# One core's hybrid S5 / RG-LRU / GLA block: more stream before the first head's transposes, a query block before z, the first norm reordered, third products at the turn

## The chip, the cores and the metric

The kernel runs on one core of a Trainium2 chip. The metric is the device time of one execution in microseconds (us), lower is better; a profile is one execution taken by the hardware profiler. Engines: PE is TensorE (matrix products), DVE is VectorE, ACT is ScalarE, POOL is GpSimd, and SP (SyncE) issues nearly all loads.

## What is computed

One block of a sequence model with 1024 latent tokens, 256 context tokens and 1024 channels, in fp32. Cut to its steps:

```python
u  = modulate(rms_norm(h, ln1_g), mod[0], mod[1])        # mod = silu(c) @ ada_w + ada_b, six parts
uc = modulate(rms_norm(hc, ln1_g), mod_c[0], mod_c[1])   # the context, its own modulation
z  = u @ w_in; zc = uc @ w_in                            # 5408 columns: S5, LRU x and gate, q, k, v, g, z, gates
s5  = s5_branch(...)       # two directions, complex diagonal scan, GELU, GLU
lru = rglru_branch(...)    # conv, sigmoid gates, two scans
gla = gla_branch(...)      # four heads, chunks of 64, decays from z
m = g[0] * (s5 @ w_br_s5) + g[1] * (lru @ w_br_lru) + g[2] * (gla @ w_br_gla)
h = h + mod[2] * (m @ w_out)
u = modulate(rms_norm(h, ln2_g), mod[3], mod[4])
h = h + mod[5] * conv_ffn(u, w_up, conv_w, conv_b, w_down)
return rms_norm(h, final_g)
```

Each mixer scans the context first and starts the latent scan from that state.

## The kernel before

Channels lie on partitions, tokens run along the free axis in two halves of 512 (j = 0, 1). Every fp32 product is three products of rounded parts: high by high, low by high, high by low (`uh`, `ul` the normed input, `wh`, `wl` a weight; the low part of a weight is a subtraction on POOL or DVE, line 221, the high part a cast on ACT, line 220). Raw weights come through two buffers (`wr`), high and low parts through three each.

**PE's order is the order of the code** (`manual_schedule` for PE). The large projections are a generator, `proj_stream`, that yields products block by block: latent blocks (`lat`), context blocks (`ctx`), value blocks (`v_steps`), the z blocks that feed the GLA decays (`z_steps`), gates and branch products. The recurrent parts are serial chains through PE, ACT, DVE and POOL; between their steps the code calls `F(name)`, which takes products worth so many us, from the table `FILL`, from the stream. A product of 512 columns counts 0.216 us there. After the last head, `fill(1e9)` takes what is left of the stream; then the merge (line 1568 ff.) multiplies the GLA output, read back from DRAM as `y0` to `y3` and split into parts, by its branch weights.

On DVE, ACT, POOL and SP a scheduler sets the order from PE's order and dependences, except in three stretches that are written out: the start of the program, where the table `START` lists the steps in the order in which every engine gets them, and two stretches around the second norm and the turn to the FFN.

The steps of `START` (methods of `Start`): `x` loads a part of the input, `sq` squares it on ACT, `sa` adds the square to the sum (on DVE, or on POOL if listed in `ONPOOL`), `rs` sums over partitions on PE, `re` and `rp` make the inverse root (DVE, then POOL's power), `rb` broadcasts it with PE, `rc` copies it. `a(r, k)` loads a piece of the modulation weights of part r, `ar(r)` multiplies it with the condition (64 small products), `at` copies the row, `ac` transposes it on PE, `am` makes scale and shift (lines 365 to 367). `un`, `u`, `ul` make the scaled input, its high part (ACT, line 323) and its low part; `m1` and `m2` are the first products of the stream's blocks that run inside the norm (line 434 ff.), `g`, `gh`, `gl` their weights.

The four places: the first head's transposes are line 1347, fed by DVE's line 1323; the z products are line 711, the value blocks' copies out of PSUM line 746, the query blocks' line 580, the LRU's sigmoid `lz` line 1000; at the turn, `q[0]` and `q[1]` are FFN products of the first two channel groups, `p3` their third products (bank `bkc`), `p4` their fourth (bank `bkd`, line 853 ff.).

Of the kernel before, what the change touches and what calls it, by code (L numbers as in the profile page):

```python
# [109 lines left out]
def tile_kernel(tc, I, out, dbg=None):  # L110
# [645 lines left out]
    def proj_stream():  # L756
# [1577 lines left out]
```

## Time and profile before

| | |
|---|---|
| median of 3 runs | 1577.93 us (1577.77 to 1577.96) |
| the profiled execution | 1578.69 us, its span 1576.6 us |
| PE busy | 1513.6 us, 96% of the span |
| DVE, ACT, POOL busy | 1096.1 (70%), 772.3 (49%), 414.6 us (26%) |
| PE's mean granted clock | 0.985 of full speed |

Times of rows count from the start of the span. A row of a timeline gives start, duration, engine, line, operation, the operands by the program's names without buffer numbers (out<-in), and in brackets how long the engine stood idle before it and who released it. Rows with a count join neighbours of one kind. A window's row gives the length, then for each engine its busy time and instructions, then the granted TensorE clock (1.00 is 2.4 GHz, 0.50 is 1.2 GHz), the busy share of the DMA engines and GB/s.

### The profile page before, as it was taken

What the parts mean: (1) busy time and instruction counts of PE and PEld (TensorE: products, weight loads), DVE (VectorE), ACT (ScalarE), POOL (GpSimd) and SP (SyncE); (2) the same over time, 40 slices, a digit from 0 to 9 for tenths busy, and PEclk for the clock granted to TensorE, in tenths of its full rate; (3) what the DMA queues carried; (4) which work ended last, traced back from release to release, by engine and by line L of the source; (5) the groups of instructions that cost most, each with busy time, mean ns of one, the idle gap of its engine ahead of it and who ended that gap; (6) DMA issues with size and microseconds to landing.
All of it is one profiled execution on the core that took longest, in us unless ns stands there. A gap on an engine that the chain in (4) does not pass through costs nothing. (4 is left out here: it accounts for less than half of the span.)

```text
span 1576.6 us, 21571 instructions
## 1 busy us (share of the span) xinstructions
PE 1513.6 (96%) x8144; PEld 1248.9 (79%) x8144; DVE 1096.1 (70%) x1645; ACT 772.3 (49%) x1223; POOL 414.6 (26%) x266
## 2 busy tenths in 40 slices
PE   5999989999996999999999989999999999999997
PEld 4788768877885888888888867778888888878887
DVE  3624379999858434642451899888888888899962
ACT  4523776785534543441332565444444444544661
POOL 2313210011124222222236335333333333000032
PEclk9999999999998999999999999999999999999998
DMA  9764533332224244131574411222222223964303
GB/s 327 256 213 132 187 129 105 117 101 59 59 67 134 77 135 148 70 88 63 172 239 145 141 60 54 94 81 80 81 81 83 93 92 109 371 240 141 101 20 107
DMA packets 93865, 199.04 MB, mean 126 GB/s; under 512 B 13505, under 2 KB 34881, under 8 KB 93633
## 3 DMA queue, kind: packets, MB, share of 16 engines
q1 hardware_dynamic: 82048, 181.75, 34.3%
q10 hardware_dynamic: 11712, 15.91, 2.9%
q8 instruction: 64, 1.05, 0.3%
q14 instruction: 41, 0.33, 0.1%
HBM read 159.11 MB, written 38.52 MB: 125 GB/s over the span
## 5 line engine op out<-in xcount | busy, mean ns | idle before, releaser
L221 POOL TENSOR_TENSOR wl<-wr,wh 128x1024 fp32r<-128x1024 f32 (+1 forms) x78 | 164.2, 2105 | 477.1 <-ACT wh L220 432.8
L220 ACT CAST wh<-wr 128x1024 fp32r<-128x1024 f32 (+2 forms) x87 | 77.1, 891 | 146.2 <-issue 41.3
L221 POOL TENSOR_TENSOR wp<-tmp,wp 128x512 fp32r<-128x512 f32 x44 | 75.2, 1726 | 217.6 <-ACT wp L220 217.6
L534 PE MATMUL ma<-uh,wh 128*128 128x512 f32 x272 | 116.9, 430 | 0.7 <-ACT pt L809 0.7
L534 PE MATMUL mb<-uh,wh 128*128 128x512 f32 x272 | 106.7, 392 | 0.0
L536 PE MATMUL ma<-ul,wh 128*128 128x512 f32 x272 | 106.7, 392 | 0.0
L536 PE MATMUL mb<-ul,wh 128*128 128x512 f32 x272 | 106.7, 392 | 0.0
L538 PE MATMUL mb<-uh,wl 128*128 128x512 f32 x272 | 106.2, 391 | 0.0
L538 PE MATMUL ma<-uh,wl 128*128 128x512 f32 x272 | 105.9, 389 | 0.0
L220 ACT CAST wp<-tmp 128x512 fp32r<-128x512 f32 x78 | 46.5, 619 | 91.4 <-DVE tmp L1648 91.2
L1714 DVE SCALAR_TENSOR_TENSOR ca<-gv,vec,ca 128x1023 f32<-128x1023 f32 (+2 forms) x66 | 62.2, 967 | 23.8 <-ACT ca L1706 23.6
L220 ACT CAST wp<-hd 128x512 fp32r<-128x512 f32 x88 | 52.8, 618 | 49.4 <-PE bkd L2023 26.3
L220 ACT CAST wp<-wr 128x512 fp32r<-128x512 f32 x97 | 58.2, 620 | 32.5 <-DMA wr<-in_wdn_dram 17.1
L1717 DVE SCALAR_TENSOR_TENSOR ca<-gv,vec,ca 128x1023 f32<-128x1023 f32 (+2 forms) x66 | 71.1, 1100 | 0.1
L1378 DVE SCALAR_TENSOR_TENSOR gl<-gl,gl 128x128 f32<-128x128 f32 x72 | 31.2, 433 | 53.1 <-ACT gl L1376 35.6
L534 PEld LDWEIGHTS ma<-uh,wh 128*128 128x128 f32 x272 | 51.3, 189 | 15.4 <-issue 5.2
L221 DVE TENSOR_TENSOR wp<-hd,wp 128x512 fp32r<-128x512 f32 x88 | 60.8, 708 | 1.2 <-ACT wp L220 1.0
L538 PEld LDWEIGHTS ma<-uh,wl 128*128 128x128 f32 x272 | 51.2, 188 | 11.3
L536 PEld LDWEIGHTS ma<-ul,wh 128*128 128x128 f32 x272 | 51.2, 188 | 11.3
L536 PEld LDWEIGHTS mb<-ul,wh 128*128 128x128 f32 x272 | 51.2, 188 | 11.2
L538 PEld LDWEIGHTS mb<-uh,wl 128*128 128x128 f32 x272 | 51.1, 188 | 11.4
L534 PEld LDWEIGHTS mb<-uh,wh 128*128 128x128 f32 x272 | 51.4, 189 | 9.6 <-issue 1.4
(643 smaller groups left out, 4606.3 us busy)
## 6 DMA issues: line engine op xcount, KB each, us to landing
wa<-in_ada_dram SPq DMA_DIRECT2D x96, 256.0 KB
wr<-in_wup_dram SPq DMA_DIRECT2D x46, 512.0 KB
wr<-in_win_dram SPq DMA_DIRECT2D x40, 512.0 KB
wr<-in_wdn_dram SPq DMA_DIRECT2D x22, 512.0 KB
hd<-hid SPq DMA_DIRECT2D x22, 512.0 KB
hid<-ca SPq DMA_DIRECT2D x21, 512.0 KB
wr<-in_wout_dram SPq DMA_DIRECT2D x16, 512.0 KB
tmp<-in_wdn_dram SPq DMA_DIRECT2D x22, 256.0 KB
```

Of the source, the lines that this page charges most:

```text
L220: S.copy(h, src)
L221: lo.tensor_tensor(l, src, f32(h), OP.subtract)
L534: PE.matmul(p[j], h[:, kk], uh[j][:, k], start=f, stop=False)
L536: PE.matmul(p[j], h[:, kk], ul[j][:, k], start=False, stop=False)
L538: PE.matmul(p[j], l[:, kk], uh[j][:, k], start=False, stop=e)
L1378: self.last = V.scalar_tensor_tensor(Sd[:, step], Sd[:, step - 1], self.dec[:, step:step + 1], Sd[:, step], OP.mult, OP.add)
L1714: V.scalar_tensor_tensor(a[:, t0_ + 1:t0_ + 1 + n1], x[:, o:o + n1], fw[0], a[:, t0_ + 1:t0_ + 1 + n1], OP.mult, OP.add)
L1717: V.scalar_tensor_tensor(a[:, t0_ + c - 1:t0_ + n - 1], x[:, o + c:o + n], fw[2], a[:, t0_ + c - 1:t0_ + n - 1], OP.mult, OP.add)
```

## The change

It does four things, and takes no arithmetic away.

- `START` is written in another order, and `ar` is split: pieces 0 to 5 of a part's products stand apart from pieces 6 and 7. The first part's six pieces now come before the broadcast `rb(0)`, the second part's before the second column sums `rs(1)`; the latent halves of input tiles 2 and 3 for j = 0 get their `un`, `u`, `ul` before those for j = 1; the later squares of the second half come after the first `m1`. `ONPOOL` is gone, so `sa` for k = 2, 4, 6 of the second half is on DVE. The square of tile 2 gets a buffer of its own; `sp` and `sf` are not called.
- The second query block (`qsp[1]`, weight 6) moves from before the key blocks of the context to after the first value blocks, right ahead of `z_steps`; its weight moves in the list of loads with it.
- `F("gtr0")`, 13.0 us of stream, ahead of the first head's transposes.
- `q[1].p3()` moves ahead of `q[0].p4()`.

```diff
@@ -72,6 +72,7 @@
         'glu': [22.0],
+        'gtr0': [13.0],
         'gtr': [3.37, 4.7, 3.88, 4.43],
@@ -83,8 +84,7 @@
-ONPOOL = [('sq', 2, 1), ('sq', 4, 1), ('sq', 6, 1)]
...
@@ -308,10 +308,11 @@
-    def ada_rows(r, p):
-        for k, w in enumerate(ada.pop(r)):
+    def ada_rows(r, p, k0=0, k1=KT):
+        for k in range(k0, k1):
+            w = ada[r][k]
@@ -338,8 +339,8 @@
-        def ar(r):
-            ada_rows(r, psm[:, r * 128:(r + 1) * 128])
+        def ar(r, k0, k1):
+            ada_rows(r, psm[:, r * 128:(r + 1) * 128], k0, k1)
@@ -387,12 +388,21 @@
-                t = sqs[k, j] = t0([128, 512], "sq", 3)
+                t = sqs[k, j] = t0([128, 512], "sq" if k != 2 else "sqp", 3 if k != 2 else 1)
...
-            (G if ("sq", k, j) in ONPOOL else V).tensor_tensor(accs1[j], accs1[j], sqs[k, j], OP.add)
+            V.tensor_tensor(accs1[j], accs1[j], sqs[k, j], OP.add)
@@ -762,18 +772,18 @@
-        wsrc.extend([win[i] for i in (35, 36, 37, 0, 5, 6, 3, 4)] + vsrc)
+        wsrc.extend([win[i] for i in (35, 36, 37, 0, 5, 3, 4)] + vsrc + [win[6]])
...
-        for b in range(2):
-            yield from lat(lambda p: out_rows(p, qsp[b]))
+        yield from lat(lambda p: out_rows(p, qsp[0]))
         for b in range(2):
             yield from ctx(lambda p: out_rows([p], ksp[b]))
         yield from v_steps([0, 1])
+        yield from lat(lambda p: out_rows(p, qsp[1]))
         yield from z_steps()
@@ -1495,6 +1505,7 @@
         if h == 0:
+            F("gtr0")
             F("gtr")
             head.transposed()
@@ -1914,10 +1925,10 @@
+    q[1].p3()
     q[0].p4()
     q[0].gate()
     q[0].out()
-    q[1].p3()
     q[1].p4()
```

Lines after the first hunk move by 1 to 11 (the broadcast copy of the first norm and what follows): line 1347 is line 1357 of the changed kernel.

How the instructions move, at three places.

**ACT ahead of the z products.** `lz` is the LRU's sigmoid, `lt` and `lw` its gates and decays, `pt` a copy out of PSUM (a value block's on line 746 before; the query block's on line 590 of the change), the row of line 707 or 717 the copy of the first z product. Before:

```order
L982 ACTIVATE lw313_2045<-la312_2042 128x1280
L972 ACTIVATE lt306_1980<-sm310_2024,hba_1480 128x512
L220 CAST wh386_2345<-wr385_2343 128x1024
L220 CAST wh389_2351<-wr388_2349 128x1024
L972 ACTIVATE lt306_1980<-sm311_2039,hba_1480 128x256
L984 ACT_TABLE_LOAD
L984 ACTIVATE lw313_2045<-lw313_2045 128x1280
L746 COPY pt315_2059<-mb308_1990 128x512
L972 ACT_TABLE_LOAD
L972 ACTIVATE lt314_2052<-sm317_2073,hba_1480 128x512
L747 DMA vsp_681<-pt315_2059 128x2x256
```

Now:

```order
L982 ACTIVATE lt307_2011<-sm308_2018,hba_1480 128x512
L1010 ACTIVATE lz295_1925<-lz295_1925 128x1024
L992 ACTIVATE lw312_2048<-la311_2045 128x1280
L982 ACTIVATE lt307_2011<-sm309_2033,hba_1480 128x512
L590 COPY pt314_2056<-ma299_1938 128x512
L590 COPY pt315_2059<-mb300_1939 128x512
L982 ACTIVATE lt307_2011<-sm310_2042,hba_1480 128x256
L994 ACT_TABLE_LOAD
L994 ACTIVATE lw312_2048<-lw312_2048 128x1280
L591 DMA qsp_680<-pt314_2056 128x512
L591 DMA qsp_680<-pt315_2059 128x512
L982 ACT_TABLE_LOAD
```

The value block's copy stood behind two casts, the table load and the square root; the query block's two copies stand before table load and root, and the two casts (`wh386`, `wh389`) have gone further up.

**PE ahead of the first head's transposes** (line 1347, now 1357; `ma`, `mb` the two halves of a stream block, `sm` the transposes). Before:

```order
L538 MATMUL ma912_4943<-uh0_109,wl870_4766 128x512
L538 MATMUL mb913_4944<-uh1_110,wl870_4766 128x512
L1347 MATMUL sm915_4964<-con_71,gl899_4909 128x128 x4
L1347 MATMUL sm916_4970<-con_71,gl899_4909 128x128 x4
L1347 MATMUL sm917_4976<-con_71,gl899_4909 128x128 x2
L534 MATMUL ma912_4943<-uh0_109,wh869_4765 128x512
```

Now, the last six rows before the first stream block ends and the next begins, and the rows at the transposes:

```order
L546 MATMUL ma912_4943<-ul0_111,wh869_4765 128x512
L546 MATMUL mb913_4944<-ul1_112,wh869_4765 128x512
L548 MATMUL ma912_4943<-uh0_109,wl870_4766 128x512
L548 MATMUL mb913_4944<-uh1_110,wl870_4766 128x512
L544 MATMUL ma919_5005<-uh0_109,wh876_4825 128x512
L544 MATMUL mb920_5006<-uh1_110,wh876_4825 128x512
```

```order
L548 MATMUL ma919_5005<-uh0_109,wl877_4826 128x512
L548 MATMUL mb920_5006<-uh1_110,wl877_4826 128x512
L1357 MATMUL sm922_5038<-con_71,gl899_4909 128x128 x4
L1357 MATMUL sm923_5044<-con_71,gl899_4909 128x128 x4
L1357 MATMUL sm924_5050<-con_71,gl899_4909 128x128 x2
L544 MATMUL ma919_5005<-uh0_109,wh876_4825 128x512
```

Before, 18 stream products stood between the S5 output's products and the transposes, all of one block; now 78 stand there, 48 that end this block and 30 of the next, with the next weight.

**DVE in the first norm** (`mods` scale and shift, `x` the scaled input, `ul` the low part, rows on line 395, now 396, the sums of squares of the second half). Before:

```order
L347 COPY t046_249<-sm12_126 128x128
L395 TENSOR_TENSOR t044_243<-t044_243,t045_247 128x512
L365 TENSOR_TENSOR mods_124<-sm11_125,ab1_104 128x4
L366 TENSOR_TENSOR mods_124<-mods_124,vec_69 128x4
L367 TENSOR_TENSOR mods_124<-sm11_125,vec_69 128x4
L320 SCALAR_TENSOR_TENSOR x1_89<-x1_89,mods_124,t025_139 128x512
L320 SCALAR_TENSOR_TENSOR x2_90<-x2_90,mods_124,t025_139 128x512
L395 TENSOR_TENSOR t044_243<-t044_243,t048_257 128x512
L326 SCALAR_TENSOR_TENSOR ul0_111<-x1_89,mods_124,uh0_109 128x512
L326 SCALAR_TENSOR_TENSOR ul0_111<-x2_90,mods_124,uh0_109 128x512
```

Now:

```order
L396 TENSOR_TENSOR t044_233<-t044_233,t045_237 128x512
L348 COPY t047_253<-sm12_126 128x128
L396 TENSOR_TENSOR t044_233<-t044_233,t046_251 128x512
L366 TENSOR_TENSOR mods_124<-sm11_125,ab1_104 128x4
L367 TENSOR_TENSOR mods_124<-mods_124,vec_69 128x4
L368 TENSOR_TENSOR mods_124<-sm11_125,vec_69 128x4
L321 SCALAR_TENSOR_TENSOR x1_89<-x1_89,mods_124,t025_139 128x512
L321 SCALAR_TENSOR_TENSOR x2_90<-x2_90,mods_124,t025_139 128x512
L327 SCALAR_TENSOR_TENSOR ul0_111<-x1_89,mods_124,uh0_109 128x512
L327 SCALAR_TENSOR_TENSOR ul0_111<-x2_90,mods_124,uh0_109 128x512
L396 TENSOR_TENSOR t044_233<-t044_233,t048_273 128x512
L396 TENSOR_TENSOR t044_233<-t044_233,t049_276 128x512
```

A sum no longer stands between the scaled inputs and their low parts, and all sums of the second half from k = 3 on stand in one row behind them.

## Rows read from the trace of the kernel before

**Rows 1.** PE's waits over the whole run: line, releaser, us in total, times, longest.

```profile
PE sm L1347 <- DVE gl L1323: 12.6, 1, 12.6
PE ma L434 <- ACT uh L323: 4.9, 1, 4.9
PE mb L711 <- ACT pt L746: 4.8, 1, 4.8
```

**Rows 2.** Windows of core 0: busy us per engine, granted PEclk, DMA share, GB/s.

```profile
27.20:32.20 5.00, 4.94 (x12) 3.89 (x13) 2.71 (x4) 2.16 (x6) 1.42 (x2) 0.50 1.05 387
215.70:220.00 4.30, 4.30 (x10) 2.27 (x10) 3.81 (x2) 2.17 (x3) 0.00 (x0) 0.50 0.47 166
509.70:513.50 3.80, 3.76 (x14) 3.47 (x15) 3.35 (x2) 0.97 (x3) 2.68 (x1) 0.50 0.12 13
953.50:957.20 3.70, 3.70 (x10) 2.92 (x11) 3.58 (x5) 3.11 (x5) 3.70 (x4) 0.57 0.00 0
40.00:60.00 20.00, 19.07 (x139) 15.36 (x140) 19.93 (x30) 10.04 (x18) 8.65 (x7) 1.00 0.95 342
280.00:300.00 20.00, 20.00 (x144) 17.33 (x143) 20.00 (x36) 12.72 (x21) 1.98 (x2) 1.00 0.31 105
```

**Rows 3.** PE's timeline at the first head's transposes: start us, us, line, operands, idle before.

```profile
492.83 0.39 PE L534 MATMUL ma<-uh,wh 128*128 128x512 f32 x1
...
496.70 0.39 PE L538 MATMUL mb<-uh,wl 128*128 128x512 f32 x1
509.74 2.39 PE L1347 MATMUL sm<-con,gl 128*128 128x128 f32 x10 [12.65 <-DVE gl L1323]
```

**Rows 4.** POOL's timeline, the next stream weight's split.

```profile
484.31 2.71 POOL L221 TENSOR_TENSOR wl<-wr,wh 128x1024 fp32r<-128x1024 f32 x1 [8.73 <-ACT wh L220]
```

**Rows 5.** PE's timeline at the first product of the merge.

```profile
770.78 0.39 PE L290 MATMUL mm<-y0h,wh 128*128 128x512 f32 x1
```

**Rows 6.** DVE's timeline, the low parts of the merge's third and fourth operands.

```profile
761.44 1.23 DVE L221 TENSOR_TENSOR y2l<-yr,y2h 128x1024 fp32r<-128x1024 f32 x1 [1.88 <-DMA wr<-in_wbr_dram]
764.79 1.23 DVE L221 TENSOR_TENSOR y3l<-yr,y3h 128x1024 fp32r<-128x1024 f32 x1 [2.12 <-ACT y3h L220]
```

**Rows 7.** ACT's timeline before the second z product.

```profile
205.12 1.06 ACT L1000 ACTIVATE lz<-lz 128x1024 f32<-128x1024 f32 x1 [3.48 <-DVE lz L999]
...
215.06 0.57 ACT L746 COPY pt<-mb 128x512 f32<-128x512 f32 x1
```

**Rows 8.** PE's timeline, the second z product.

```profile
215.68 0.69 PE L711 MATMUL mb<-uh,tmp 128*64 128x512 f32 x1 [4.78 <-ACT pt L746]
```

**Rows 9.** DVE's timeline, two weight splits in the LRU.

```profile
211.29 2.36 DVE L221 TENSOR_TENSOR wl<-wr,wh 128x1024 fp32r<-128x1024 f32 x2
```

**Rows 10.** PE's timeline at the start of the program.

```profile
15.85 2.07 PE L279 MATMUL sm<-con,t 128*128 128x128 f32 x8 [1.35 <-POOL t L408]
17.85 3.64 PE L316 MATMUL sm<-wa,c 128*32 128x128 f32 x64
...
27.26 0.80 PE L434 MATMUL ma<-uh,wh 128*128 128x512 f32 x1 [4.86 <-ACT uh L323]
```

**Rows 11.** DVE's timeline at the start of the program.

```profile
22.63 1.25 DVE L366 TENSOR_TENSOR mods<-mods,vec 128x4 f32<-128x4 f32 x1
23.80 0.15 DVE L367 TENSOR_TENSOR mods<-sm,vec 128x4 f32<-128x4 f32 x1
...
25.25 0.68 DVE L395 TENSOR_TENSOR t<-t,t 128x512 f32<-128x512 f32 x1
```

**Rows 12.** ACT's timeline at the start of the program.

```profile
25.96 0.63 ACT L391 ACTIVATE t<-x 128x512 f32<-128x512 f32 x1 [1.44 <-DVE t L395]
```

**Rows 13.** PE's timeline at the turn to the FFN.

```profile
953.48 0.47 PE L853 MATMUL bkd<-T4h,wp 128*128 128x512 f32 x1 [3.15 <-DVE gv L1688]
```

**Rows 14.** ACT's timeline at the turn to the FFN.

```profile
952.53 0.58 ACT L1684 COPY gv<-bkc 128x512 f32<-128x512 f32 x1
```

**Rows 15.** SP's timeline, weight loads of the LRU's end.

```profile
212.54 32.41 SPq L211 DMA_DIRECT2D wr<-in_wv_dram  x4
```

More of the change, by code (lines that the diff above doesn't have):

```diff
@@ new lines @@
+START = [('x', 0, 0), ('sq', 0, 0), ('x', 1, 0), ('sq', 1, 0), ('x', 2, 0), ('sq', 2, 0), ('sa', 1, 0), ('x', 3, 0), ('sq', 3, 0), ('sa', 2, 0), ('x', 4, 0), ('sq', 4, 0), ('sa', 3, 0), ('x', 5, 0), ('sq', 5, 0), ('sa', 4, 0), ('x', 6, 0), ('sq', 6, 0), ('sa', 5, 0), ('x', 7, 0), ('sq', 7, 0), ('sa', 6, 0), ('sa', 7, 0), ('rs', 0), ('a', 0, 0), ('a', 0, 1), ('a', 0, 2), ('a', 0, 3), ('a', 0, 4), ('a', 0, 5), ('ar', 0, 0, 6), ('re', 0), ('rp', 0), ('a', 0, 6), ('a', 0, 7), ('g', 0), ('gh', 0, 0), ('rb', 0), ('gh', 0, 1), ('gl', 0, 0), ('gh', 0, 2), ('x', 0, 1), ('sq', 0, 1), ('gl', 0, 1), ('x', 1, 1), ('sq', 1, 1), ('gl', 0, 2), ('ar', 0, 6, 8), ('rc', 0), ('sa', 1, 1), ('x', 2, 1), ('sq', 2, 1), ('at', 0), ('ac', 0), ('sa', 2, 1), ('am', 0), ('un', 0, 0), ('un', 1, 0), ('u', 0, 0), ('u', 1, 0), ('ul', 0, 0), ('m1', 0, 0), ('ul', 1, 0), ('x', 3, 1), ('sq', 3, 1), ('x', 4, 1), ('sq', 4, 1), ('sa', 3, 1), ('m2', 0, 0), ('x', 5, 1), ('sq', 5, 1), ('m1', 1, 0), ('sa', 4, 1), ('x', 6, 1), ('sq', 6, 1), ('sa', 5, 1), ('x', 7, 1), ('sq', 7, 1), ('a', 1, 0), ('a', 1, 1), ('a', 1, 2), ('a', 1, 3), ('a', 1, 4), ('a', 1, 5), ('ar', 1, 0, 6), ('sa', 6, 1), ('sa', 7, 1), ('m2', 1, 0), ('a', 1, 6), ('a', 1, 7), ('g', 1), ('gh', 1, 0), ('gh', 1, 1), ('gl', 1, 0), ('ar', 1, 6, 8), ('gh', 1, 2), ('rs', 1), ('at', 1), ('gl', 1, 1), ('gl', 1, 2), ('ac', 1), ('re', 1), ('rp', 1), ('am', 1), ('a', 2, 0), ('a', 2, 1), ('a', 2, 2), ('a', 2, 3), ('a', 2, 4), ('a', 2, 5), ('ar', 2, 0, 6), ('un', 2, 0), ('un', 3, 0), ('u', 2, 0), ('rb', 1), ('u', 3, 0), ('ul', 2, 0), ('a', 2, 6), ('a', 2, 7), ('g', 2), ('gh', 2, 0), ('ul', 3, 0), ('gh', 2, 1), ('gl', 2, 0), ('gh', 2, 2), ('ar', 2, 6, 8), ('rc', 1), ('gl', 2, 1), ('m1', 2, 0), ('at', 2), ('un', 0, 1), ('gl', 2, 2), ('un', 1, 1), ('u', 0, 1), ('ac', 2), ('m2', 2, 0), ('un', 2, 1), ('u', 1, 1), ('a', 3, 0), ('a', 3, 1), ('a', 3, 2), ('a', 3, 3), ('a', 3, 4), ('a', 3, 5), ('ar', 3, 0, 6), ('am', 2), ('u', 2, 1), ('ul', 0, 1), ('m1', 0, 1), ('ul', 1, 1), ('ul', 2, 1), ('a', 3, 6), ('a', 3, 7), ('g', 3), ('gh', 3, 0), ('gh', 3, 1), ('ar', 3, 6, 8), ('gl', 3, 0), ('un', 3, 1), ('gh', 3, 2), ('m2', 0, 1), ('gl', 3, 1), ('at', 3), ('u', 3, 1), ('un', 4, 0), ('m1', 1, 1), ('gl', 3, 2), ('ul', 3, 1), ('u', 4, 0), ('ac', 3), ('un', 5, 0), ('m2', 1, 1), ('am', 3), ('u', 5, 0), ('m1', 3, 0), ('ul', 4, 0), ('ul', 5, 0), ('m1', 2, 1), ('un', 4, 1), ('un', 5, 1), ('u', 4, 1), ('m2', 3, 0), ('un', 6, 0), ('u', 5, 1), ('m2', 2, 1), ('ul', 4, 1), ('u', 6, 0), ('m1', 3, 1), ('ul', 5, 1), ('ul', 6, 0), ('m1', 4, 0), ('un', 7, 0), ('m2', 3, 1), ('un', 6, 1), ('u', 7, 0), ('m2', 4, 0), ('un', 7, 1), ('u', 6, 1), ('m1', 5, 0), ('ul', 7, 0), ('u', 7, 1), ('ul', 6, 1), ('m1', 4, 1), ('ul', 7, 1), ('m2', 5, 0), ('m2', 4, 1), ('m1', 5, 1), ('m1', 6, 0), ('m2', 5, 1), ('m2', 6, 0), ('m1', 6, 1), ('m2', 6, 1), ('mz',)]
@@ L394, in sa, with sp, sf @@
         def sa(k, j):
-            (G if ("sq", k, j) in ONPOOL else V).tensor_tensor(accs1[j], accs1[j], sqs[k, j], OP.add)
+            V.tensor_tensor(accs1[j], accs1[j], sqs[k, j], OP.add)
+        @staticmethod
+        def sp(k, j):
+            G.tensor_tensor(sqs[2, j], sqs[2, j], sqs[k, j], OP.add)
+        @staticmethod
+        def sf(j):
+            Start.sa(2, j)
         @staticmethod
```

1 line of the change is left out of this document (removed).

## The prediction

> **What bounds the kernel now.** I read the page's busy shares first: TensorE (PE) is busy 96% of a span of 1576.6 us, so everything that this change can win is in the other 4%, some 63 us, and in stretches where PE's clock is at the lower of its two levels. The view of PE's waits comes next; three of its rows stand where the change does something [rows 1]: 12.6 us before the first head's transposes (on VectorE, DVE), 4.9 us before the first product of the first norm and 4.8 us before the second z product (both on ScalarE, ACT). Third, the granted clock by stretch [rows 2]: 0.50, which is 1.2 of 2.4 GHz, in the 5.0 us after the second of these waits, the 4.3 us after the third and the 3.8 us after the first. A 512-column product moves on by 0.228 us at full clock (492.83 to 496.70, 17 steps [rows 3]), and at half clock takes twice that, so half of each stretch is lost: 2.5, 2.15 and 1.9 us. Last, the timelines of PE and of the engines it waits for at each place.
>
> PE's order is written by hand, so products are not re-sorted at run time: a wait removed in front of PE shortens the whole as long as the engines behind it move along.
>
> **C, 13 us of stream ahead of the first head's transposes.** Before, PE runs out of stream 18 products after 492.83, and waits 12.65 us to 509.74 for DVE's product at L1323 [rows 3]. The change puts 60 more products there, 60 x 0.228 = 13.7 us; they end at 492.83 + 78 x 0.228 = 510.6, 0.9 us after the transposes could begin. Thirty of the 60 use the weight tile that is in use, thirty the next one, which POOL split at 484.31 in 2.71 us [rows 4]. ACT, DVE and POOL keep their order up to the transposes, so DVE's chain stays where it is. The wait of 12.65 us goes and the 1.9 us of half clock behind it: 14.5 us at most. None of it shows at the place: it comes back after the last head, where 60 products less are left to drain.
>
> What is late next is the merge. After the last head 126 stream products stood before the merge, now 66. The merge started at 770.78 [rows 5] and would start 13.7 us earlier, at 757.1 of that clock. Its third and fourth operands y2l and y3l were split by DVE at 761.44 and 764.79, 1.23 us each [rows 6], 4.8 us before the merge began. A step of the merge is six products, 1.37 us, and the low operand is the second product of its step, so they are wanted at 757.1 + 2 x 1.37 + 0.23 = 760.1 and 761.4. With the old times PE would stand until 766.0: 4.6 us in all. SyncE (SP) now has no weight load between the store of the last head and the loads of y, so these go out about 1 us earlier, and y3 needs no weight load to pass; but one weight load, waiting for a split on GpSimd (POOL), now stands ahead of that store. Bounds 0 and 4.6; I take 2.0. **C: 14.5 - 2.0 = 12.5 us.**
>
> **B, one query block between value products and z.** Before, the last block ahead of z is a value block; its copy out of PSUM stands on ACT behind the LRU's casts, a table load and a square root, and starts at 215.06 only [rows 7]. PE needs that buffer for its second z product at 215.68 - 4.78 = 210.9 [rows 8]. After the change the block ahead of z is the query block, and its two copies stand ahead of table load and root. What can still hold them is the LRU's sigmoid `lz`, which ACT ran at 205.12 after waiting 3.48 us for DVE [rows 7]: two weight splits, 2.36 us together [rows 9], now stand on DVE ahead of the scans that feed it. Then `lz` would start at 207.5 and, with 1.06 for itself and about 3 us for the two LRU steps and two copies that follow, the second copy ends near 211.6, against a need at 210.9: 0.7 us of wait. If DVE has the splits done in its own idle time it is 0. I take 0.4. The 2.15 us of half clock go with the wait. **B: 4.8 + 2.15 - 0.4 = 6.5 us**; bounds 0 (copies late after all) and 7.
>
> **A, the first norm.** Before: the broadcast of the root starts at 15.85, the 64 small products of the first modulation part at 17.85, they take 3.64 us and end at 21.49; the first product of the norm comes at 27.26, after 4.86 us of idle [rows 10]. Now 48 of the 64 go ahead of the broadcast, while POOL's power runs: 14.5 (15.85 - 1.35, where the column sums end) + 48/64 x 3.64 = 17.2, broadcast 2.0, the last 16 0.9: 20.1, 1.4 us earlier. From there to the first product it took 27.26 - 21.49 = 5.8 us. In it DVE's L366 took 1.25 us where its neighbours take 0.15 [rows 11], beside a sum on POOL that the change takes from there (1.1 us), and ACT put a Square at 25.96 ahead of the first u, which waited for a sum of DVE that ended at 25.93 [rows 11, 12]; the u steps now stand ahead of those squares (some 1.9 us). So the first product comes about 1.4 + 1.1 + 1.9 = 4.4 us earlier. SP's loads keep their order. Three sums of 0.68 us move from POOL to DVE [rows 11], 2.0 us, and DVE is busy 19.93 of 20 us from 40 to 60 [rows 2], so part of the gain may end there: -1 to 5; nearest is the 4.4 less half of the sums. **A: 3.5 us.** The idle ahead of the product shrinks from 4.86 to about 2.9 us, and I keep half clock behind it, since 3.15 us of idle at the turn [rows 13] were followed by a granted 0.57 [rows 2].
>
> On that clock the Trainium skill ("TensorE: Matmul & The Clock Gate", section "What's actually happening") says that the throttled state is the default and that sustained activity releases it. Both rows agree with that; they don't settle whether 2.9 us with small products around them is idle enough, so the other outcome is a rival below, worth the 2.5 us lost there before.
>
> **D, the third products of the second pair ahead of the fourth of the first.** PE waits 3.15 us to 953.48 [rows 13]. The third products that now come first write the bank that ACT copies out at 952.53 for 0.58 us [rows 14], and use a weight split that ends a little later. So PE waits to 953.1 at the earliest and some 954 at the latest; DVE has work waiting in either order. **D: -0.3 us**, bounds -0.9 and +0.4.
>
> **Give-back.** A and B bring PE to the S5 stage 10 us earlier. DVE is busy 20.00 of 20 us at 280 to 300 [rows 2] and PE has almost no wait there; DVE's chain begins on a load that SP issues behind weight loads, one of which now stands later, so it should start as much earlier. I take 1 us lost, bounds 0 and 10.
>
> **Sum.** 3.5 + 6.5 + 12.5 - 0.3 - 1.0 = 21.2 us. The profiled execution took 1578.69 us, so 1557.5; it lies 0.76 above the median of the runs (1577.93), so I predict 1556.7 us. A measurement of this kernel can tell about 0.2% from no change, 3.2 us.
>
> **Rivals.**
> 1. *The merge stands.* y2 and y3 come as late as before, 4.6 us, and half clock after it costs another 1 (3.7 us at 0.57 after the turn's wait lost 1.6 [rows 2]): 3.6 us worse, 1560.3. For it: both splits were late already [rows 6]. Against: the loads are issued earlier. 0.13.
> 2. *The first norm gives nothing*, because DVE, full from 40 to 60, or the transfers, 0.95 of their share there [rows 2], set its end: 1560.2. 0.11.
> 3. *All of it is hidden, and the first norm keeps the full clock*: A 4.4 + 2.5, B 7, C 14.5, nothing given back: 28.4 us, 1549.5. The clock rule named above is the reason for its 2.5. For it: the gap is shorter than any that half clock follows in rows 2. 0.07.
> 4. *S5 does not move*: DVE starts its chain when it did, and the 10 us of A and B become a wait of PE: 1566. Against: DVE's order there has nothing new. 0.04.
> 5. *Slower.* The two weight splits that now stand ahead of the LRU's scans on DVE wait for late weight loads; scans, sigmoid, copies, z and S5 all queue behind them. One weight load in this place did stand 32.41 us in SP's group of issues [rows 15]. It makes the change slower than before from a lateness of 21.2 + 3.2 = 24.4 us. Against: in SP's order the two loads now stand ahead of that wait. At 30 us: 1587; from 18 to 24 us there would be no difference. 0.04.
> 6. *The extra stream is not there in time*: the products put ahead of the transposes wait for weights or for PSUM, and C is worth nothing: 1569. Against: the split of rows 4 ends long before 503, where the second thirty begin. 0.01.
>
> **How the numbers follow.** The forecast has 0.60. Rivals 1 and 2 lie at 1560, both together near 1564, and rival 3 at 1549.5; the range from 1551.0 to 1564.5 takes in the forecast with the bounds of C and A, and rivals 1 and 2. Left out are 3, 4, 5 and 6, 0.16. Faster by over 0.2%: all but 5, 0.96; of rival 5, 0.01 within 0.2% and 0.03 slower.
>
> **What would show it.** Right: no wait on the transposes of the first head over 2 us and a granted 1.00 around them; no wait of 4.8 us on the second z product; the first product of the norm near 23 us; a new wait of 1 to 3 us on y2l or y3l in the merge; an unchanged wait near 3 us at the turn, now on third products. Wrong: a wait on the transposes as long as A and B together (S5 did not move), over 4 us at the merge, or a first product of the norm after 25 us.

## The result and the profile after

| | before | after |
|---|---|---|
| median of 4 runs each, side by side | 1577.95 us (1577.77 to 1578.85) | 1555.95 us (1553.71 to 1556.22) |
| ratio, 95% interval | | 0.9856 [0.9839, 0.9873] |
| profiled execution | 1578.69 us | 1556.22 us |

22.0 us faster, 1.4%; the forecast was 1556.7, the range 1551.0 to 1564.5. PE has 3.2 us less work in the records and 19 us less idle time. The page after, span and busy times:

```profile
span 1554.4 us, 21567 instructions
PE 1510.4 (97%) x8144; PEld 1244.1 (80%) x8144; DVE 1090.0 (70%) x1648; ACT 774.7 (50%) x1223; POOL 403.1 (26%) x263
```

PE's waits after (in total, times, longest); the rows to compare with are [rows 1]:

```profile
PE bkc L863 <- ACT gv L1695: 2.8, 1, 2.8
PE bkb L864 <- DVE wp L221: 2.4, 1, 2.4
PE ma L444 <- ACT uh L324: 2.4, 1, 2.4
...
PE sm L291 <- DVE s L225: 1.6, 1, 1.6
...
PE mm L290 <- ACT y2h L220: 1.0, 1, 1.0
```

The wait on the transposes (12.6, now L1357) and the one on the second z product (4.8, now L721) are gone, the first norm's (L444) is half as long, and the merge (`mm`) has waits that it hadn't. L291's wait on `s`, the end of S5, was 1.1 before: 0.5 us of what S5 takes back.

PE's order is rigid, so the same instruction can be found in both traces. Its start before less its start after is the lead, and where the lead changes, the time was won or lost:

| PE instruction | before | after | lead |
|---|---|---|---|
| first product of the first norm | 27.26 | 22.82 | 4.44 |
| start of the stream behind the norm | 72.48 | 68.31 | 4.17 |
| second z product | 215.68 | 205.53 | 10.15 |
| first modulation product behind z | 221.84 | 210.08 | 11.76 |
| a middle S5 block | 465.07 | 453.34 | 11.73 |
| stream ahead of the transposes | 492.83 | 481.59 | 11.24 |
| merge, first product | 770.78 | 744.56 | 26.22 |
| merge, second block | 776.27 | 753.16 | 23.11 |
| first FFN products | 920.92 | 897.75 | 23.17 |
| last product | 1568.09 | 1545.29 | 22.80 |

So in this pair of profiles A gave 4.2, B 7.6, S5 took back 0.5, C gave 15.0 to the merge's first product and the merge took back 3.1, and the turn and all behind it changed the time by 0.4. The granted clock after, by stretch (length, PE busy, clock, DMA share, GB/s), against [rows 2]:

```profile
22.80:25.60 2.80, 2.78 (x7) 0.50 1.05 386
200.00:220.00 20.00, 19.56 (x144) 1.00 0.35 128
500.00:520.00 20.00, 19.86 (x128) 1.00 0.41 138
740.00:760.00 20.00, 17.75 (x75) 1.00 0.57 193
930.00:935.00 5.00, 4.79 (x14) 0.66 0.00 0
```

Of the stretches at half clock one is gone at z and one at the transposes, the first norm's is 2.8 us long and no longer 5.0, and the turn's has stayed.

**C at its place.** PE's timeline after, answering to [rows 3]:

```profile
499.30 1.25 PE L1357 MATMUL sm<-con,gl 128*128 128x128 f32 x10
```

DVE's product, the releaser of the wait before, ran here:

```profile
496.54 2.18 DVE L1333 TENSOR_TENSOR gl<-gl,gl 128x1280 f32<-128x1280 f32 x1 [2.75 <-ACT gl L1326]
```

It ends at 498.72, PE arrives at 499.30: 0.6 us late, where 0.9 was worked out.

**The merge.** PE after, where [rows 5] had no wait:

```profile
744.56 0.39 PE L290 MATMUL mm<-y0h,wh 128*128 128x512 f32 x1
...
747.08 0.40 PE L292 MATMUL mm<-y1h,wl 128*128 128x512 f32 x1
748.46 0.51 PE L290 MATMUL mm<-y2h,wh 128*128 128x512 f32 x1 [0.98 <-ACT y2h L220]
749.77 0.50 PE L291 MATMUL mm<-y2l,wh 128*128 128x512 f32 x1 [0.81 <-DVE y2l L221]
...
751.90 0.50 PE L291 MATMUL mm<-y3l,wh 128*128 128x512 f32 x1 [0.47 <-DVE y3l L221]
```

The brackets add up to 2.26 us, but the block takes 3.11 us longer than before. A bracket counts from the modelled end of the product ahead, which is longer (0.39) than the step to the next (0.23): 747.08 to 748.46 is 1.38, so 1.15 is lost where the bracket shows 0.98. SP after, in the same place:

```profile
734.07 1.58 SPq L1560 DMA_DIRECT2D yr<-yosp  x2
...
743.87 1.55 SPq L1560 DMA_DIRECT2D yr<-yosp  x2
```

y0 and y1 are loaded at 734.07; y2 and y3 only at 743.87, since `yr` has two buffers and DVE split the first of them at 742.61 for 1.23 us. The prediction named SP's queue and the weight load in it as what holds these loads; it was the buffers. (In the kernel before it was both: y2's load went out at 755.67, at the end of the first of these splits, y3's at 758.17, behind a weight load.)

**B at its place.** ACT after, against [rows 7]:

```profile
199.93 1.04 ACT L1010 ACTIVATE lz<-lz 128x1024 f32<-128x1024 f32 x1
...
204.47 0.60 ACT L590 COPY pt<-mb 128x512 f32<-128x512 f32 x1
```

The second copy ends at 205.07 and the second z product starts at 205.53 without a wait. `lz` came 5.2 us earlier than before, 1.0 more than A's lead at the stream. The two weight splits that moved ahead of the scans on DVE did take their time, but it came back. DVE after, with the two splits and the product behind the scans:

```profile
191.20 1.22 DVE L221 TENSOR_TENSOR wl<-wr,wh 128x1024 fp32r<-128x1024 f32 x1
...
192.94 1.20 DVE L221 TENSOR_TENSOR wl<-wr,wh 128x1024 fp32r<-128x1024 f32 x1
...
196.90 1.22 DVE L1012 TENSOR_TENSOR lt<-lt,lt 128x1024 f32<-128x1024 f32 x1
```

The same product before, and the weight split that POOL ran beside it:

```profile
199.27 2.87 POOL L221 TENSOR_TENSOR wl<-wr,wh 128x1024 fp32r<-128x1024 f32 x1 [4.09 <-ACT wh L220]
199.98 3.24 DVE L1002 TENSOR_TENSOR lt<-lt,lt 128x1024 f32<-128x1024 f32 x1
```

From DVE's product ahead of the scans (L986, now L996, at 195.34 and 189.79) to their end (199.95 and 196.40) it takes 6.6 us now and took 4.6 before: the splits cost 2.0. The product behind the scans takes 1.22 us and no longer 3.24, because POOL splits nothing beside it: 2.0 won. In noB and onlyC (below), where the query block stands in its old place, it took 3.2 us beside a POOL split again, in all other runs 1.2 without one.

### The profile page after: what moved, and what is told of

Same layout as the page of the kernel before. It is cut to its first block, busy times and chain, and to the rows that moved or that the text cites. A ratio compares the mean times of both kernels' runs of the same rounds, so it can differ in the third digit from the quotient of the medians.

```text
span 1554.4 us, 21567 instructions
## 1 busy us (share of the span) xinstructions
PE 1510.4 (97%) x8144; PEld 1244.1 (80%) x8144; DVE 1090.0 (70%) x1648; ACT 774.7 (50%) x1223; POOL 403.1 (26%) x263
## 5 line engine op out<-in xcount | busy, mean ns | idle before, releaser
L221 POOL TENSOR_TENSOR wl<-wr,wh 128x1024 fp32r<-128x1024 f32 (+1 forms) x78 | 160.9, 2064 | 450.4 <-ACT wh L220 426.6
```

Source lines behind the costliest of these rows:

```text
L221: lo.tensor_tensor(l, src, f32(h), OP.subtract)
```

## The experiments

Eleven runs; the totals in one table, each against runs of the kernel before on the same chip. A median of 4 runs is good to about 0.15%, 2.5 us, so what is smaller is read from the leads at the place and not from totals.

| run | median (range) us | ratio to before [95%] |
|---|---|---|
| noA | 1557.21 (1556.66 to 1560.82) | 0.9874 [0.9857, 0.9891] |
| noB | 1562.70 (1561.15 to 1565.51) | 0.9904 [0.9886, 0.9921] |
| noC | 1568.93 (1568.14 to 1571.09) | 0.9944 [0.9930, 0.9958] |
| noD | 1556.90 (1553.96 to 1556.99) | 0.9863 [0.9846, 0.9879] |
| onlyC | 1563.69 (1562.94 to 1565.34) | 0.9918 [0.9905, 0.9932] |
| g8 | 1570.30 (1569.68 to 1572.47) | 0.9963 [0.9950, 0.9977] |
| g16 | 1568.79 (1565.99 to 1570.44) | 0.9941 [0.9929, 0.9952] |
| yr4 | 1554.43 (1552.97 to 1555.80) | 0.9858 [0.9844, 0.9871] |
| sumsPool | 1558.78 (1555.51 to 1561.88) | 0.9885 [0.9870, 0.9900] |
| noDyr4 | 1557.66 (1554.47 to 1559.41) | 0.9870 [0.9855, 0.9884] |
| chg2 | 1556.67 (1554.47 to 1557.76) | 0.9865 [0.9850, 0.9879] |

**One part undone at a time.** noA is the change with the start of before:

```diff
+ONPOOL = [('sq', 2, 1), ('sq', 4, 1), ('sq', 6, 1)]
...
-    def ada_rows(r, p, k0=0, k1=KT):
+    def ada_rows(r, p):
...
-            V.tensor_tensor(accs1[j], accs1[j], sqs[k, j], OP.add)
+            (G if ("sq", k, j) in ONPOOL else V).tensor_tensor(accs1[j], accs1[j], sqs[k, j], OP.add)
```

and `START` with it.

> The changed kernel with the first norm's old order (old START, unsplit ar, three sums on POOL). Theory, the parts add up and each lead is carried to the end: the start of the stream falls back by about 4.0 us (68.3 to 72.4), every later place by the same, 1560 us; the first product of the norm waits 4.9 us again. Rival, the lead of the first norm is lost later in DVE's S5 chain or at the merge: 1556 us, the first head's transposes then stand where they stand now, near 499.3.

Measured 1557.21, between the two. Its first product waits 4.70 us again. Its lead at the stream is 1.35 (after: 4.17), and the difference of 2.8 us is still there behind z (8.96 against 11.76), at the merge (23.76 against 26.22) and at the FFN (20.38 against 23.17): nothing of A is hidden later. What differs is A itself, which is less in the mean of several profiles (below).

noB:

```diff
-        wsrc.extend([win[i] for i in (35, 36, 37, 0, 5, 3, 4)] + vsrc + [win[6]])
+        wsrc.extend([win[i] for i in (35, 36, 37, 0, 5, 6, 3, 4)] + vsrc)
...
-        yield from lat(lambda p: out_rows(p, qsp[0]))
+        for b in range(2):
+            yield from lat(lambda p: out_rows(p, qsp[b]))
...
-        yield from lat(lambda p: out_rows(p, qsp[1]))
         yield from z_steps()
```

> The changed kernel with the second query block back in front of the key blocks of the context. Theory: the wait of 4.8 us on the second z product returns with 4.3 us at half clock behind it, and S5 begins some 7.5 us later: 1563.5 us. Rival, the lead of this part is mostly used up by S5's DVE chain: 1558 us or less, and PE's waits in S5 are smaller than in the changed kernel.

Measured 1562.70, 6.75 more than the change. PE's row at z, as in [rows 8]:

```profile
211.06 0.61 PE L721 MATMUL mb<-uh,tmp 128*64 128x512 f32 x1 [4.71 <-ACT pt L756]
```

noC takes the line `'gtr0': [13.0]` and `F("gtr0")` out.

> The changed kernel without the 13 us of stream ahead of the first head's transposes. Theory: PE waits about 12.6 us there (DVE's chain has moved with PE), half clock follows, and no wait stands in the merge: 1568 us. Rival, DVE's chain had not followed PE's lead of 11 us: a wait of 20 us or more there, 1575 us or more.

Measured 1568.93, 13.0 more than the change. PE stands again, 10.5 us earlier than in [rows 3] and as long, and the merge has no wait:

```profile
499.24 1.12 PE L1356 MATMUL sm<-con,gl 128*128 128x128 f32 x4 [12.62 <-DVE gl L1332]
```

noD puts `q[1].p3()` back behind `q[0].out()`.

> The changed kernel with the third products of the second pair back behind the output of the first. Theory, the turn costs 0.4 us in the new order: 1555.6 us, a wait of 3.1 us on the fourth products. Rival, the new order wins the 1 us that it was put in for: 1557 us. Neither can be told from no change by the total alone, the place where PE stands 50 us after the turn tells them apart.

Measured 1556.90, 0.95 more than the change, which is within the error. The wait at the turn (the longer of the two in the first row) is 2.75 us with the old order, 2.83 in the change; the wait behind it is 1.88 us, 2.45 in the change:

```profile
PE bkd L863 <- DVE gv L1699: 3.9, 2, 2.8
...
PE bkb L864 <- DVE wp L221: 1.9, 1, 1.9
```

The four differences, 1.26 + 6.75 + 12.98 + 0.95, make 21.9 of the 22.0 us gained: within the error of medians the parts add.

**C alone** (the kernel before with the two lines of `gtr0`).

> The kernel before with the 13 us of stream ahead of the first head's transposes alone. Theory (the parts add, each on its own stretch): the wait of 12.6 us and the half clock after it go; at the merge's first product the lead over before is 14.5 to 15 us, in its first block about 3 us are given back (low parts late), and the total is 12 us shorter, near 1565.8. Rival (C leans on A and B, since a merge that starts at another place of the load queues waits otherwise): a lead at the end under 9 us or over 14.

Measured 1563.69, 13.1 less than before, where 12 was expected. Its lead grows from 3.25 us behind z to 17.97 at the merge, by 14.7, and the merge takes back 1.7, where 3 was expected: C leans on no other part. (The 3.25 are a better start than the profile of before happened to have, not an effect of C.)

**The amount of stream.** g8 writes 8.0 in place of 13.0, g16 writes 16.0.

> The change with 8 us of stream in place of 13 ahead of the transposes (some 37 products in place of 60). Theory (PE's order is rigid and DVE's chain there keeps its place): PE runs out 23 products earlier, 5.2 us, and waits some 4.7 us for the product of DVE, with a lower clock behind it that costs another 1.5 to 2.5 us; the merge starts 6 to 7 us later than in the change and its three waits (2.26 us) go, so the total is 4 to 5 us longer, near 1560.5. Rival 1 (a wait of under 5 us leaves the clock alone here): 2.5 us longer, 1558.5. Rival 2 (the drain after the last head absorbs it): no difference from the change.

> The change with 16 us of stream ahead of the transposes, some 14 products more than one block of the stream (a block is 60: 48 on the input, 12 on the branch). Theory (the amount matters twice: it covers the wait, and 60 products leave every later block boundary at the same step of the heads, where ACT is free to read the bank; any other amount moves boundaries to steps where ACT stands waiting for DVE): the transposes start about 3.2 us later than in the change with no wait and full clock, and new waits on ACT's tanh of a block appear in the heads, 1 to 7 us in all; total 1557 to 1563. Rival (only the cover of the wait counts, what is more is neither won nor lost): no wait on the tanh over 1 us, total within 1 us of the change's.

Both miss: 1570.30 (expected 1560.5) and 1568.79 (1557 to 1563), 14.3 us more than the change and 12.1 more than chg2, its run beside g16. In g8 the wait at the transposes is as expected, but more stands in the heads:

```profile
PE ma L544 <- ACT pt L819: 7.1, 2, 5.3
PE sm L1357 <- DVE gl L1333: 4.7, 1, 4.7
```

The 7.1 us are two waits; the longer one is 5.28 us to 645.95. ACT's timeline of g8 just ahead of its end:

```profile
644.73 0.22 ACT L1321 ACTIVATE gl<-gl 64x20 f32<-64x20 f32 x1 [3.68 <-DVE gl L1317]
...
645.29 0.60 ACT L819 ACTIVATE pt<-ma 128x512 f32<-128x512 f32 x1
```

And DVE's timeline there:

```profile
638.84 2.81 DVE L1313 TENSOR_TENSOR_SCAN gl<-gl,gl 64x1280 f32<-64x1280 uint8 x1
641.68 2.82 DVE L1314 TENSOR_TENSOR_SCAN gl<-gl,gl 64x1280 f32<-64x1280 uint8 x1
```

A block of the stream ended at 640.67, and its bank had to be read by ACT (L819), which stood behind the decays' exponential, which waited for DVE's two scans. In the kernel after, the same read is at 633.52, ahead of the scans. In g16 the two scans hold DVE's own accumulation (L837), the last reader of the bank:

```profile
651.13 0.80 PE L826 MATMUL mb<-yb,wh 128*128 128x512 f32 x1 [5.40 <-DVE acc L837]
```

The engine differs from the one I had expected for g16, the mechanism is the same: a block is 60 products (48 on the input, 12 on the branch), and 13 us of stream are just 60. So with 13.0 every later block of 60 ends at the step of the heads where it ended before: the copies in the heads of L809 before and L819 after stand at 645.43 and 633.52, at 662.61 and 650.69, 11.9 us apart like ACT's other work beside them. With 37 or 74 products the ends move into the scans. (The blocks ahead of these, up to 611 us, are 48 products long; their ends do move, and the lead there only falls from 12.3 to 11.9 us.) g8's 14.3 us are, by its leads, 10.2 lost by the last head (2.31 there, 12.47 in the change) and 5.2 for the 23 products that are left to drain, less 3.1 that the merge does not take back; some 2 lie behind the turn. g16 against chg2 loses 5.7 by the merge's first product (20.36 and 26.08), 3.1 more in the merge and 1.9 behind the turn. The prediction saw two of three effects of this term (cover and merge); the third, no harm in the heads, it got by luck.

**The merge's loads.** yr4 is the change with

```diff
-        t = pyp.tile([128, 1024], F32, name=nm(name), tag=name, bufs=2)
+        t = pyp.tile([128, 1024], F32, name=nm(name), tag=name, bufs=4 if name == "yr" else 2)
```

> The change with four buffers in place of two for the reloaded GLA output, so that y2 and y3 are loaded without waiting for the splits of y0 and y1. Theory (the second pair of loads waits for the first pair's splits, and that sets the merge's waits): the three waits in the merge's first block (0.98, 0.81 and 0.47 us, 2.26 together) go, and about 2.3 us of the total with them: near 1553.7 in the median, and the lead over before at the merge's second block grows from 23.1 to about 25.4 us. Rival (the loads from DRAM themselves, or ACT's and DVE's other work in front of the splits, are late): the waits stay within 0.5 us of what they were, and the time stays at 1556. Second rival: the time won at the merge is given back at the turn, whose wait grows from 2.8 to about 5 us.

At the place the theory holds in part: SP issues all four loads at 735.19, the waits on y2h and y2l go, and the merge takes back 1.23 us in place of 3.11 (2.45 in chg2, the change once more). But y3l still waits, as PE's timeline of yr4 shows:

```profile
751.12 0.50 PE L291 MATMUL mm<-y3l,wh 128*128 128x512 f32 x1 [0.93 <-DVE y3l L221]
```

DVE's timeline of yr4 ahead of it:

```profile
749.25 0.67 DVE L837 TENSOR_TENSOR acc<-acc,mb 128x512 f32<-128x512 f32 x1
749.85 1.21 DVE L221 TENSOR_TENSOR y3l<-yr,y3h 128x1024 fp32r<-128x1024 f32 x1
```

The scheduler now puts the last block's four accumulations between y2l and y3l. The wait at the turn stays 2.83 us, so the second rival fell. The total, 1554.43, can't be told from the change (ratios 0.9858 and 0.9856).

**The sums of the second half.** sumsPool is the change with

```diff
-            V.tensor_tensor(accs1[j], accs1[j], sqs[k, j], OP.add)
+            (G if (k, j) in ((2, 1), (4, 1), (6, 1)) else V).tensor_tensor(accs1[j], accs1[j], sqs[k, j], OP.add)
```

> The change with the three sums of squares of the second half back on POOL. Theory (the first norm's gain came from the order, with the u steps ahead of the squares and 48 small products ahead of the broadcast; taking the sums off POOL is about 1.1 us of it, the slow DVE product beside a POOL sum): the first product of the norm stays between 22.8 and 24.0 us, and the stream starts within 1 us of 68.3. Rival (the sums on POOL were what held it): the first product comes after 25 us and the stream starts after 70. Second rival (DVE, full from 40 to 60 us, pays for the sums): the stream starts before 67.5 and the total falls by about 1 us.

First product at 22.96, stream at 68.21: the order of steps is what A lives on. The sums on POOL cost 0.46 us ahead of the first product (2.87 us from L352 to it, 2.41 in chg2), and none of it is left at the stream; the second rival fell too. Its clock after the first product was low for twice as long (windows of PE, from the first product on):

```profile
22.96:25.96 3.00, 3.00 (x7) 0.50 1.05 388
25.96:28.96 3.00, 3.00 (x8) 0.52 1.04 387
```

and still the stream starts no later. Over the ten profiles with the new start the stream begins at 68.42 in the mean where the low stretch is short (seven) and at 68.51 where it is long (noC, g8 and this one), so half clock there cost next to nothing at the stream. Up to the FFN sumsPool is level with the change (lead 22.86 and 23.17); its total of 1558.78 comes from behind the turn, as follows.

**The turn, and the change once more.** noDyr4 joins the edits of noD and yr4; chg2 is the change itself.

> The change with the third products of the second pair back in their old place, and with four buffers for the reloaded GLA output. Theory (the new order at the turn saves 0.3 us at its own wait, but the next wait, fourth products on a weight split of DVE, grows from some 1.7 to 2.45 us and in four of seven profiles a lower clock follows it, in none of three with the old order): no lowered clock in the 40 to 50 us behind the turn, from the second norm's column sums to the end the kernel takes 704.4 us as before (704.7 to 709.6 in profiles with the new order), and the median is 1 to 2.5 us under that of the change: 1553.5 to 1555. Rival (the clock after that wait varies by chance in either order): the stretch from the second norm to the end scatters over 704 to 709 here too, and the median is that of the four buffers with the new order, 1554.4, or above.

> The change itself once more, beside the two others on the same chip. Theory (the start's profiles scatter; the order of the first norm is worth 3.5 us at its first product, and later waits follow the order of the code): first product between 22.5 and 23.1 us, stream start between 68.2 and 68.9, the same waits of 2.4 to 2.8 us at the turn and 2.45 behind it; median within 1.5 us of 1556. Rival to the theory on the turn: no wait of 2.45 us behind it, or one under 2.

chg2 came as expected: first product at 22.56, stream at 68.25, waits of 2.82 and 2.45 us at and behind the turn, median 1556.67.

The stretch from the second norm's column sums to the last product took, with the old order of the turn, 704.35, 704.62, 704.58 and 704.25 us (before, noD, onlyC, noDyr4). With the new order it took 704.34 to 705.33 in four (noC, after, chg2, yr4) and 706.5, 706.8, 707.0, 707.6 and 709.6 in five (noA, g16, g8, noB, sumsPool). All nine have the wait of 2.4 us behind the turn; the five have a low clock behind it. The window of 5 us from that product on, first of sumsPool:

```profile
981.90:986.90 5.00, 5.00 (x12) 0.50 0.30 105
```

The same window of chg2:

```profile
979.30:984.30 5.00, 5.00 (x22) 1.00 0.33 107
```

The old order gives a shorter wait here (1.55 to 2.23 us), and no low clock in four profiles. Yet the medians of noD and noDyr4 lie 1 us above the change and chg2, not 1 to 2.5 below: the expectation on totals fell. What the new order is worth stays open: the stretch is 706.3 us in the mean of nine profiles with it and 704.45 in four without, by the medians it is 1 us better, and a median is good to 2.5 us. The four buffers also brought less here: y3l waited 1.86 us in noDyr4, and in one piece, after which the clock fell (window of 5 us around it):

```profile
749.63:754.63 5.00, 3.14 (x10) 0.77 0.19 52
```

Four buffers alone are no safe gain.

## Why the prediction was right

The time was 0.75 us from the forecast, and the mechanism of A, B and C was the one named. That it came so close is in part luck: in this pair of profiles A, B, C to the merge and S5 came 0.5 to 1.1 us better than put and the merge 1.1 worse, and of the lead of 22.80 us at the last product 0.55 is gone by the end of the span. The terms (us gained; a minus is a loss):

| term | predicted | profiles | by medians |
|---|---|---|---|
| A | 3.5 | 4.2; mean of several 2.7 | 1.3 (noA) |
| B | 6.5 | 7.6; against noB 6.7 | 6.75 (noB) |
| S5 give-back | -1.0 | -0.5 | |
| C to the merge | 14.5 | 15.0; onlyC 14.7 | |
| merge | -2.0 | -3.1; chg2 -2.5 | |
| C in all | 12.5 | 11.9 | 13.0 (noC), 13.1 (onlyC) |
| D and behind | -0.3 | -0.4 | 0.95 (noD) |

- **C** was right in its parts: the wait, the half clock behind it, the 0.9 us of excess (0.6). The gain shows at the merge and not at the transposes, as said.
- **The merge** was mis-sized: 3.1 us for 2.0, and its cause was another. Old split times, moved up by 1 us, were the argument; the runs show that the loads of y2 and y3 wait for two buffers (yr4 takes the waits on y2 away). Of rival 1's 4.6 us this is two thirds; its half clock did not come in this profile, but did in those of noD and noDyr4.
- **B**: the wait on `lz` did not come, and B is near the bound 7 that was named. The reason is not DVE's idle time, which the prediction gave for this case: the splits cost DVE 2.0 us, near the 2.36 put, and a product of DVE without POOL's split beside it gave 2.0 back, which the prediction did not have. Of the 7.6 us in this pair 0.9 stands in noB too, so it is not B's.
- **A** was right in its parts, each somewhat smaller than put. The first product came at 22.82, predicted near 23. Over nine profiles with the new start (all but sumsPool) it comes at 22.67 in the mean, over three with the old one (before, noA, onlyC: 27.26, 26.15, 25.50) at 26.30: 3.6 us, where the parts made 4.4. The rows after:

```profile
14.29 2.79 PE L317 MATMUL sm<-wa,c 128*32 128x128 f32 x48
...
19.01 0.64 PE L317 MATMUL sm<-wa,c 128*32 128x128 f32 x16
20.06 0.39 PE L352 MATMUL sm<-con,t 128*128 128x8 f32 x2 [0.41 <-DVE t L348]
22.82 0.80 PE L444 MATMUL ma<-uh,wh 128*128 128x512 f32 x1 [2.37 <-ACT uh L324]
```

  and of onlyC, with the old start:

```profile
20.41 0.39 PE L352 MATMUL sm<-con,t 128*128 128x8 f32 x2 [0.42 <-DVE t L348]
25.50 0.80 PE L435 MATMUL ma<-uh,wh 128*128 128x512 f32 x1 [4.70 <-ACT uh L324]
```

  The 48 products ahead of the broadcast bring the transposing products (L352) forward by 0.9 us between the means (20.22 against 21.12; 0.35 against onlyC, 1.85 against before); 1.4 was put. From L352 to the first product it is 2.76 us here, 2.41 to 2.43 in the other eight, and 5.09 in noA and onlyC. Of these 2.7 us the sum on POOL is 0.9, where 1.1 was put. The slow L366 [rows 11] took 0.16 us in noA and in onlyC, but the cost was there all the same, one step further on. The sum on POOL and DVE's work beside it, before (L366 at 22.63, 1.25 us), then in noA:

```profile
22.60 1.26 POOL L395 TENSOR_TENSOR t<-t,t 128x512 f32<-128x512 f32 x1 [2.94 <-DVE mods L365]
```

```profile
21.75 1.26 POOL L396 TENSOR_TENSOR t<-t,t 128x512 f32<-128x512 f32 x1 [2.55 <-DVE mods L366]
21.91 2.31 DVE L321 SCALAR_TENSOR_TENSOR x<-x,mods,t 128x512 f32<-128x512 f32 x2
```

  After, without a sum on POOL, the same two scaled inputs take 0.9 us less:

```profile
21.26 1.41 DVE L321 SCALAR_TENSOR_TENSOR x<-x,mods,t 128x512 f32<-128x512 f32 x2
```

  The other 1.8 us, an estimate from these differences, is the `u` ahead of the squares, where 1.9 was put. Against this 0.9 of the 3.6 us is gone by the start of the stream (68.47 in the mean against 71.17: 2.7 us), near the 1.0 that the term took off for a busy DVE. That DVE is the reason is not shown: with the three sums off DVE again (sumsPool) the stream started at 68.21, in the others at 68.25 to 68.83.
- **The clock behind the first product** stayed at half, as forecast, and rival 3 fell: 0.50 for 2.8 us after 2.37 us of idle. On this the Trainium skill ("TensorE: Matmul & The Clock Gate", section "What's actually happening") has the throttled state as the default; the trace agrees in that the clock was low behind this idle time, though noDyr4 kept 1.00 behind 3.15 us at the turn (last section). The length of the slow stretch varies: 2.8 us here, some 6 in sumsPool behind a wait of 2.48, 5.0 before.
- **D** is the term that was thought through least. Its own wait went from 3.15 to 2.83 us, where a loss of 0.3 was put; but the old order shows 2.71 to 3.15 in four profiles and the new one 2.25 to 2.83 in nine, so this pair alone shows no gain. What the prediction did not follow is the next wait: on a product that needs DVE's weight split PE waits 2.39 to 2.45 with the new order and 1.55 to 2.23 with the old; in return a wait of 0.70 to 1.14 on fourth products behind it, at 1034.95 before, is gone. Wait by wait the sum is about nothing.

Rivals 2, 4, 5 and 6 are each against a row above: a first norm that gives 2.7 us, no wait at the transposes, `lz` early, stream in time.

## What to carry to other kernels

Filling a wait from a stream whose order is fixed has two sizes to fit: the length of the wait, and the stream's own block. Moving a whole block left the later bank hand-overs where they were; 3 us more or 5 us less than a block cost 12 and 14 us here, in waits of the heads some 150 us further on, in the merge and behind the turn. And a term read from one long row (a product of 1.25 us that its neighbours do in 0.15) should be looked for in a second profile by its cause and not by its line: there the same POOL sum held the next instruction.

## What was not expected of the hardware

The same wait does not always cost the same clock. Behind the 2.4 us at the product after the turn the granted clock was 1.00 in four profiles and 0.50 to 0.70 over 5 us in five, with one code in that stretch. (Four of the five, and one of the four, had waited another 0.47 to 0.93 us some 9 us ahead of it; noA, the fifth, had not. What decides is open.) At the turn itself a wait of 3.15 us was followed by 0.57 before [rows 2] and by 1.00 in noDyr4:

```profile
931.60:936.60 5.00, 5.00 (x22) 1.00 0.00 0
```

In the merge it was the same: in noD it was 0.66 over the 5 us behind waits of 1.06 and 0.81 us, and 1.00 behind waits of 1.48, 0.81 and 0.20 in noA and 0.98, 0.81 and 0.47 in the change. So a short wait has two prices here, and one profile shows one of them. The window of noD:

```profile
749.38:754.38 5.00, 4.71 (x14) 0.66 0.14 50
```

The window of noA:

```profile
752.02:757.02 5.00, 4.08 (x16) 1.00 0.17 60
```

The longer waits, 4.68 in g8, 4.71 in noB and 5.28 in g8, had a low clock behind them (0.58, 0.57 and 0.50 over 3 to 4 us).

A POOL instruction can hold a DVE instruction beside it. The DVE product behind the scans took 3.23 to 3.24 us in the three profiles in which a POOL split ran beside it (before, noB, onlyC) and 1.21 to 1.22 in the ten in which none did. In the first norm the DVE instruction that took two operands from SBUF and started beside the POOL sum ended 0.02 us behind the sum's end in before and in sumsPool, while one that reads PSUM (`sm`) took 0.15 us beside the same sum in noA.
